# A hybrid encoder trunk on one core: gates and branch projections with tokens stationary and 512 weight columns moving

## The chip, the cores and the metric

One NeuronCore of a Trainium2 chip runs the whole kernel. The metric is the device time in microseconds (us) from the start to the end of one execution; lower is better. Engines are named as the profile does: PE is the matrix engine TensorE, with PEld its loads of stationary operands; DVE is VectorE, ACT is ScalarE, POOL is GpSimd, and SP is the engine whose queue issues most DMAs. SBUF is the on-chip working memory of 128 partitions, PSUM the small accumulation memory that PE writes.

## What is computed

Two layers act on 256 tokens of 1,024 features, all in fp32. In each layer four token mixers (three attentions and a convolution) give four branches of 256 features. What this case is about is the joining of the four:

```python
proj = jnp.einsum('bsnc,ncd->bsnd', branches, w_branch)
gates = jax.nn.sigmoid(h @ w_gate + b_gate).reshape(b, s, N_BRANCH, D_MODEL)
x = x + jnp.sum(gates * proj, axis=2) @ w_o

hf = rms_norm(x, g_ffn)
x = x + jnp.square(jax.nn.relu(hf @ w_up)) @ w_down
```

Here `h` is the RMS-normed input, `w_gate` has 1,024 x 4,096 entries, `w_branch` four times 256 x 1,024, and `w_o` 1,024 x 1,024.

## The kernel before

**Weights and matmuls.** All weights are streamed, in tiles of 128 partitions x 1,024 floats (512 KB). `weights` (L102) loads such a tile by a DMA of SP into `raw` (five buffers), lets ACT round it to `hi` (L114) and DVE subtract to `lo = raw - hi` (L115); `hi` and `lo` have four buffers each. While `share[1]` is 2, which is so during attention, every second `lo` is made by POOL. Activations are split into the same two parts. A product is three matmuls (`mm3`, L120 to L124): high by high, and the two mixed ones, in a reduced-precision type. Whichever operand is stationary has 128 columns; the other one moves.

**Gates.** `gates(g)` (L712) makes two blocks of 128 output features for all 256 tokens: the weights are stationary, the 256 tokens of `xg` move, eight blocks of the contraction and three matmuls each, 24 per weight tile (`mtile`, L341). DVE multiplies the two blocks by the tokens' norm factor (L717) into `Z`, which holds features in the partitions; `sigmoids` (L719) adds the bias as a per-partition scalar and applies the sigmoid on ACT.

**Branches.** `branch(m)` (L724) does the four projections of one block of 128 output features, 24 matmuls of 256 moving tokens. DVE multiplies them by the gates (L737), POOL adds the four in two steps (L738, L739), ACT and DVE split the sum into its two parts `y` (L740, L741), which stand ready as the stationary operand of the output projection.

**Output projection.** From L779 on, tokens are stationary and 512 columns of `w_o` move (`tokens`, L761), 12 matmuls per weight tile, accumulated in four PSUM tiles `po`; the result is added to the stream `X` (`joined`, L771), and `to_features` (L296) turns X by fp32 transposes for the MLP.

**Order.** PE's instructions run in the order in which the program names them. The other engines' and the DMA queue's orders are set at build time by a scheduler that gives each engine, in program order of priority, what its model says is ready; an engine then runs its list in that order. During attention, `tick` (L333) is called behind each weight tile and runs the next list of steps of `side`: scores, transposes and weighted values of a head, pieces of the convolution. There are 31 such lists per layer, 13 of them used up before the gates begin, so 18 gate tiles share PE with attention. Behind that, L744 to L758 put one `branch` after each `gates`.

**PSUM.** There are eight banks: four `mm` (pool `pmm`, through `new_ps`), one `sc` for scores, one `pv` for weighted values, and two `ms` for transposes and small things.

Of the kernel before, what the change touches and what calls it, by code (L numbers as in the profile page):

```python
# [17 lines left out]
F32 = mybir.dt.float32  # L18
# [6 lines left out]
P = 128  # L25
# [17 lines left out]

C_GMIX, C_GFFN, C_BGATE, C_GQ, C_GKV, C_DW, C_BDW, C_GLN, C_BLN, C_BF = 0, 8, 16, 48, 50, 51, 113, 115, 117, 119
NSMALL = 123

# [23 lines left out]
@with_exitstack  # L70
def hybrid_trunk(ctx: ExitStack, tc: tile.TileContext, xT, xtok, pos, small, gfin, abias, w_lat, w_v, w_in, w_uq, w_ukv,
                 w_gate, w_br, w_o, w_up, w_dn, out):
# [17 lines left out]
    def nm(s):  # L90
        count[0] += 1
        return f"{s}_{count[0]}"
# [33 lines left out]
    def cols(pair, i):  # L126
        return pair[0][:, i * P:(i + 1) * P], pair[1][:, i * P:(i + 1) * P]
# [197 lines left out]
    for l in range(L):  # L325
        s = sm[l]

        def col(c):
            return s[:, c:c + 1]
# [377 lines left out]


        Z = [big.tile([P, 16, T], F32, tag="big", name=nm("Z")) for _ in range(2)]
        y = [None, None]  # L710

        def gates(g):  # L712
            ps = new_ps("pgt")
            for i in range(2):
                mtile(ps[:, i * T:(i + 1) * T], w_gate[l, 2 * g + i], xg)
            i = 2 * g % 16
            nc.vector.tensor_tensor(Z[g // 8][:, i:i + 2, :], ps2(ps), bc(rb, 2), op=ALU.mult)  # L717

        def sigmoids(m):  # L719
            for i in range(4 * m, 4 * m + 4):  # L720
                zt = Z[i // 16][:, i % 16, :]
                after(nc.scalar.activation(zt, zt, AF.Sigmoid, bias=col(C_BGATE + i)), last_exp[0])

        def branch(m):  # L724
            if m == 0:
                y[:] = [act.tile([P, 8, T], F32R, tag="qk1", name=nm("yh")),
                        act.tile([P, 8, T], F32R, tag="qk2", name=nm("yl"))]
            w = weights(w_br[l, m])
            yt = tmp.tile([P, 4, T], F32, tag="y4", name=nm("yt"))
            for a in range(2):  # L730
                ps = new_ps("pbr")
                for n in range(2):
                    for k in range(2):
                        i = 2 * (2 * a + n) + k
                        mm3(ps[:, n * T:(n + 1) * T], cols(w, i), part(br, i), k == 0, k == 1)
                i = (4 * m + 2 * a) % 16
                nc.vector.tensor_tensor(yt[:, 2 * a:2 * a + 2, :], ps2(ps), Z[m // 4][:, i:i + 2, :], op=ALU.mult)  # L737
            nc.gpsimd.tensor_tensor(yt[:, 0:2, :], yt[:, 0:2, :], yt[:, 2:4, :], op=ALU.add)  # L738
            nc.gpsimd.tensor_tensor(yt[:, 0, :], yt[:, 0, :], yt[:, 1, :], op=ALU.add)  # L739
            nc.scalar.copy(y[0][:, m, :], yt[:, 0, :])  # L740
            nc.vector.tensor_tensor(y[1][:, m, :], yt[:, 0, :], y[0][:, m, :], op=ALU.subtract)  # L741

        nbr = -1
        for g in range(16):  # L744
            gates(g)
            if side:
                continue
            share[1] = 0
            if nbr < 0:
                conv_silu(last_exp[0])  # L750
            else:
                branch(nbr)
            nbr += 1
            sigmoids(nbr)
        for m in range(nbr, KT):
            branch(m)
            if m + 1 < KT:
                sigmoids(m + 1)  # L758


        def tokens(ps, st, w, j, first, last):  # L761
# [3 lines left out]
        def block(pair, k, b):  # L765
            return pair[0][:, k, b * P:(b + 1) * P], pair[1][:, k, b * P:(b + 1) * P]

        xg2 = new_xg()
        po = {(b, h): new_ps("po") for h in range(2) for b in range(NB)}

# [4 lines left out]

        def gffn(k):
            return col(C_GFFN + k)

        for kp, h in ((0, 0), (0, 1), (1, 0), (1, 1), (2, 0), (2, 1), (3, 0), (3, 1)):  # L779
            w = weights(w_o[l, kp, h])  # L780
            for b in range(NB):
                for j in range(2):
                    k = 2 * kp + j
                    tokens(po[b, h], block(y, k, b), w, j, k == 0, k == KT - 1)
                if kp == 3:
                    joined(b, h)
# [176 lines left out]
```

## Time and profile before

| | |
|---|---|
| median of three runs | 844.81 us (844.40 to 846.23) |
| the profiled execution | 843.17 us |
| its span in the trace | 841.4 us |
| mean granted clock of PE | 0.998 of full |
| PE, DVE, ACT, POOL busy | 98%, 68%, 53%, 18% of the span |
| bytes moved by DMA | 145.55 MB, 173 GB/s on average |

The span is what the trace covers; the execution's own time has 1.8 us around it. Busy shares are averages over stages with different limits, and a PE shown busy is not PE at its peak, since its matmuls are pipelined and overlap in the records. Start-to-start distances tell its pace.

### The profile page before, as it was taken

The numbers are of one execution on the slowest core, as the hardware profiler recorded it, in microseconds if no ns is written. First come the engines' busy times: TensorE is split into PE (matmuls) and PEld (weight loads), VectorE is DVE, ScalarE is ACT, GpSimd is POOL, SyncE is SP. The second block draws the span as 40 slices with busy tenths as digits, with TensorE's granted clock in tenths as the row PEclk, the third lists the DMA queues.
The fourth block names the chain that finished last, engine by engine and source line by source line (L and its number), as shares of the span: only waits on it lengthen the run. The fifth ranks groups of instructions, "written<-read, shape, count | busy, mean of one in ns | idle before, by whom it ended". The sixth has DMA issues, their size and how long they took to land.

```text
span 841.4 us, 14516 instructions
## 1 busy us (share of the span) xinstructions
PE 823.5 (98%) x5646; PEld 757.9 (90%) x5646; DVE 570.1 (68%) x948; ACT 449.5 (53%) x757; POOL 153.0 (18%) x156
## 2 busy tenths in 40 slices
PE   8999999999999999999999999999999999999996
PEld 7879999999889999999899899999998899999995
DVE  7899984787675555555578899557866655555554
ACT  6755546654464444444485664485445554545443
POOL 6534232133200000000014332312331000000000
PEclk9999999999999999999999999999999999999999
DMA  8765343455556555656554534345555555555531
GB/s 278 223 211 173 125 140 128 160 184 192 161 165 201 179 196 181 193 181 197 165 174 160 190 129 149 130 133 173 193 176 200 174 183 194 188 189 181 194 127 50
DMA packets 42549, 145.55 MB, mean 173 GB/s; under 512 B 5104, under 2 KB 7408, under 8 KB 42352
## 3 DMA queue, kind: packets, MB, share of 16 engines
q1 hardware_dynamic: 41904, 142.98, 52.7%
q10 hardware_dynamic: 576, 1.64, 0.6%
q8 instruction: 44, 0.72, 0.4%
q14 instruction: 25, 0.20, 0.1%
HBM read 143.55 MB, written 1.05 MB: 172 GB/s over the span
## 4 chain that ended last, share of the span: by engine, by line
PE 91%; DVE 5%; issue 2%; POOL 1%; DMA 1%; ACT 0%; SPq 0%; POOLq 0%; DVEq 0%; ACTq 0%
PE pgt L122 7%; PE pgt L123 7%; PE pgt L124 7%; PE pu L123 7%; PE pu L124 7%; PE pd L123 7%; PE pu L122 7%; PE pd L122 7%; PE pd L124 7%; PE S L555 2%; DVE lo L115 2%; PE pqk L122 2%; PE pPV L593 2%; PE pqk L123 2%; PE pqk L124 2%; PE po L122 2%
## 5 line engine op out<-in xcount | busy, mean ns | idle before, releaser
L115 DVE TENSOR_TENSOR lo<-raw,hi 128x1024 fp32r<-128x1024 f32 (+3 forms) x241 | 298.4, 1241 | 196.6 <-ACT hi L114 194.4
L114 ACT CAST hi<-raw 128x1024 fp32r<-128x1024 f32 (+2 forms) x273 | 278.4, 1024 | 266.9 <-issue 208.7
L122 PE MATMUL pgt<-xgh,hi 128*128 128x256 f32 x512 | 149.5, 292 | 0.0
L122 PE MATMUL pu<-xgh,hi 128*128 128x256 f32 x512 | 144.9, 283 | 0.7 <-ACT xgh L293 0.7
L123 PE MATMUL pu<-xgl,hi 128*128 128x256 f32 x512 | 145.1, 283 | 0.3
L124 PE MATMUL pu<-xgh,lo 128*128 128x256 f32 x512 | 144.9, 283 | 0.0
L123 PE MATMUL pgt<-xgl,hi 128*128 128x256 f32 x512 | 144.7, 283 | 0.0
L124 PE MATMUL pgt<-xgh,lo 128*128 128x256 f32 x512 | 144.7, 283 | 0.0
L123 PE MATMUL pd<-hi,u 128*128 128x512 f32 x256 | 100.5, 393 | 1.1 <-DVE u L804 1.1
L122 PEld LDWEIGHTS pu<-xgh,hi 128*128 128x128 f32 x512 | 98.0, 191 | 3.4 <-ACT xgh L293 1.1
L122 PE MATMUL pd<-hi,u 128*128 128x512 f32 x256 | 100.7, 393 | 0.4 <-ACT u L803 0.4
L123 PEld LDWEIGHTS pu<-xgl,hi 128*128 128x128 f32 x512 | 98.0, 191 | 3.0 <-DVE xgl L294 0.7
L124 PE MATMUL pd<-lo,u 128*128 128x512 f32 x256 | 99.6, 389 | 0.0
L122 PEld LDWEIGHTS pgt<-xgh,hi 128*128 128x128 f32 x512 | 97.9, 191 | 0.8 <-issue 0.3
L123 PEld LDWEIGHTS pgt<-xgl,hi 128*128 128x128 f32 x512 | 98.1, 192 | 0.4
L124 PEld LDWEIGHTS pu<-xgh,lo 128*128 128x128 f32 x512 | 98.0, 191 | 0.0
L124 PEld LDWEIGHTS pgt<-xgh,lo 128*128 128x128 f32 x512 | 97.9, 191 | 0.0
L115 POOL TENSOR_TENSOR lo<-raw,hi 128x1024 fp32r<-128x1024 f32 (+1 forms) x32 | 77.2, 2414 | 110.7 <-ACT hi L114 106.1
L491 DVE SCALAR_TENSOR_TENSOR cacc<-up,sm,cacc 128x256 f32<-128x256 f32 x120 | 77.4, 689 | 0.0
L124 PEld LDWEIGHTS pd<-lo,u 128*128 128x128 f32 x256 | 48.1, 188 | 10.4
L123 PEld LDWEIGHTS pd<-hi,u 128*128 128x128 f32 x256 | 48.3, 189 | 9.4 <-DVE u L804 1.7
L122 PEld LDWEIGHTS pd<-hi,u 128*128 128x128 f32 x256 | 48.3, 189 | 9.2 <-ACT u L803 0.8
(254 smaller groups left out, 1356.8 us busy)
## 6 DMA issues: line engine op xcount, KB each, us to landing
raw<-in_w_gate SPq DMA_DIRECT2D x64, 512.0 KB, 3.8
raw<-in_w_up SPq DMA_DIRECT2D x64, 512.0 KB, 4.1
raw<-in_w_dn SPq DMA_DIRECT2D x64, 512.0 KB, 3.9
raw<-in_w_in SPq DMA_DIRECT2D x23, 512.0 KB, 4.2
raw<-in_w_br SPq DMA_DIRECT2D x16, 512.0 KB, 3.6
raw<-in_w_o SPq DMA_DIRECT2D x16, 512.0 KB, 4.4
raw<-in_w_v SPq DMA_DIRECT2D x8, 512.0 KB, 4.3
raw<-in_w_lat SPq DMA_DIRECT2D x8, 210.0 KB, 4.9
```

Source lines behind the costliest of these rows:

```text
L114: cut = nc.scalar.copy(hi[:, c:c + w], raw[:, c:c + w])
L115: done = eng.tensor_tensor(lo[:, c:c + w], raw[:, c:c + w], hi[:, c:c + w], op=ALU.subtract)
L122: nc.tensor.matmul(ps, sh, mh, start=first, stop=False)
L123: nc.tensor.matmul(ps, *((sl, mh) if late_mov else (sh, ml)), start=False, stop=False)
L124: nc.tensor.matmul(ps, *((sh, ml) if late_mov else (sl, mh)), start=False, stop=last)
L491: ins = nc.vector.scalar_tensor_tensor(cacc[:, c, :], up[:, c, j:j + T], wcol, cacc[:, c, :], op0=ALU.mult, op1=ALU.add)
L555: nc.tensor.matmul(sl, q[:, b * P:(b + 1) * P], k[:, 0:n], start=True, stop=True)
L593: nc.tensor.matmul(po[o:o + 64, 0:T], v[:, 0, vo:vo + HD], pts[:, 0:T], start=True, stop=False)
```

## The change

Gates and branch projections change operands: the tokens become stationary (128 at a time, two blocks `b`) and 512 weight columns move, as the output projection does already. The weights are laid out for it on the host. `gates(c, i)` makes the gate of branch `i` for the half `c` of the output features from four weight tiles, with `tick` behind each of them; DVE scales by the per-token norm factor and adds the bias in one operation. As the bias now lies along the free axis, it comes as a tile of 128 x 512 floats (256 KB) per gate by a DMA of its own, into one buffer, and leaves the table `small`, which shrinks from 123 to 91 columns. `sigmoids(c)` runs over 1,024 elements per partition. `branch(c, i)` projects one branch onto 512 features of both token blocks, in PSUM banks of the `sc`, `pv` and `ms` pools; DVE multiplies into `Z` in place; POOL adds the branches 1 and 2 to the sum in `Z[c][:, 0]`, DVE adds branch 3. The sum has tokens in its partitions, so `turned(c)` turns it by 8 fp32 transposes per half into `y`, copied by ACT and subtracted by DVE. The last four branch tiles are interleaved with output tiles. The core of the diff (numbering of the table's columns and some of the host's layout left out):

```diff
-def hybrid_trunk(ctx: ExitStack, tc: tile.TileContext, xT, xtok, pos, small, gfin, abias, w_lat, w_v, w_in, w_uq, w_ukv,
+def hybrid_trunk(ctx: ExitStack, tc: tile.TileContext, xT, xtok, pos, small, gfin, bgate, abias, w_lat, w_v, w_in, w_uq, w_ukv,
...
@@ -705,80 +705,99 @@
         qk(4, True)
         qk(6, False)
 
-
-        Z = [big.tile([P, 16, T], F32, tag="big", name=nm("Z")) for _ in range(2)]
-        y = [None, None]
-
-        def gates(g):
-            ps = new_ps("pgt")
-            for i in range(2):
-                mtile(ps[:, i * T:(i + 1) * T], w_gate[l, 2 * g + i], xg)
-            i = 2 * g % 16
-            nc.vector.tensor_tensor(Z[g // 8][:, i:i + 2, :], ps2(ps), bc(rb, 2), op=ALU.mult)
-
-        def sigmoids(m):
-            for i in range(4 * m, 4 * m + 4):
-                zt = Z[i // 16][:, i % 16, :]
-                after(nc.scalar.activation(zt, zt, AF.Sigmoid, bias=col(C_BGATE + i)), last_exp[0])
-
-        def branch(m):
-            if m == 0:
+        def tokens(ps, st, w, j, first, last):
+
+            mm3(ps, st, (w[0][:, j * 512:(j + 1) * 512], w[1][:, j * 512:(j + 1) * 512]), first, last, late_mov=True)
+
+        def block(pair, k, b):
+            return pair[0][:, k, b * P:(b + 1) * P], pair[1][:, k, b * P:(b + 1) * P]
+
+
+        Z = [big.tile([P, 4, NB, 512], F32, tag="big", name=nm("Z")) for _ in range(2)]
+        y = []
+
+        def gates(c, i):
+            ps = [new_ps("pgt") for _ in range(NB)]
+            bg = tmp.tile([P, 512], F32, tag="bg", name=nm("bg"), bufs=1)
+            for kp in range(4):
+                w = weights(w_gate[l, c, i, kp])
+                if kp == 0:
+                    nc.sync.dma_start(bg, bgate[l, c, i])
+                for b in range(NB):
+                    for j in range(2):
+                        k = 2 * kp + j
+                        tokens(ps[b], block(xg, k, b), w, j, k == 0, k == KT - 1)
+                tick()
+            for b in range(NB):
+                nc.vector.scalar_tensor_tensor(Z[c][:, i, b, :], ps[b], rc[:, b:b + 1], bg, op0=ALU.mult, op1=ALU.add)
+
+        def sigmoids(c):
+            for i in range(4):
+                after(nc.scalar.activation(Z[c][:, i], Z[c][:, i], AF.Sigmoid), last_exp[0])
+
+        def branch(c, i):
+            pools = (((psc, "sc"), (ppv, "pv")), ((pms, "ms"), (pms, "ms")))[i % 2]
+            ps = [pool.tile([P, 512], F32, tag=tag, name=nm("pbr")) for pool, tag in pools]
+            w = weights(w_br[l, c, i])
+            for b in range(NB):
+                for j in range(2):
+                    tokens(ps[b], block(br, 2 * i + j, b), w, j, j == 0, j == 1)
+                nc.vector.tensor_tensor(Z[c][:, i, b, :], ps[b], Z[c][:, i, b, :], op=ALU.mult)
+                if i == 3:
+                    nc.vector.tensor_tensor(Z[c][:, 0, b, :], Z[c][:, 0, b, :], Z[c][:, 3, b, :], op=ALU.add)
+            if i in (1, 2):
+                nc.gpsimd.tensor_tensor(Z[c][:, 0], Z[c][:, 0], Z[c][:, i], op=ALU.add)
+
+        def turned(c):
+
+            if c == 0:
                 y[:] = [act.tile([P, 8, T], F32R, tag="qk1", name=nm("yh")),
                         act.tile([P, 8, T], F32R, tag="qk2", name=nm("yl"))]
-            w = weights(w_br[l, m])
-            yt = tmp.tile([P, 4, T], F32, tag="y4", name=nm("yt"))
-            for a in range(2):
-                ps = new_ps("pbr")
-                for n in range(2):
-                    for k in range(2):
-                        i = 2 * (2 * a + n) + k
-                        mm3(ps[:, n * T:(n + 1) * T], cols(w, i), part(br, i), k == 0, k == 1)
-                i = (4 * m + 2 * a) % 16
-                nc.vector.tensor_tensor(yt[:, 2 * a:2 * a + 2, :], ps2(ps), Z[m // 4][:, i:i + 2, :], op=ALU.mult)
-            nc.gpsimd.tensor_tensor(yt[:, 0:2, :], yt[:, 0:2, :], yt[:, 2:4, :], op=ALU.add)
-            nc.gpsimd.tensor_tensor(yt[:, 0, :], yt[:, 0, :], yt[:, 1, :], op=ALU.add)
-            nc.scalar.copy(y[0][:, m, :], yt[:, 0, :])
-            nc.vector.tensor_tensor(y[1][:, m, :], yt[:, 0, :], y[0][:, m, :], op=ALU.subtract)
-
-        nbr = -1
-        for g in range(16):
-            gates(g)
+            for pr in range(2):
+                pt = pms.tile([P, 512], F32, tag="ms", name=nm("pyt"))
+                for j in range(2):
+                    o = (2 * pr + j) * P
+                    for b in range(NB):
+                        nc.tensor.transpose(pt[:, j * T + b * P:j * T + (b + 1) * P], Z[c][:, 0, b, o:o + P], ident)
+                ks = slice(4 * c + 2 * pr, 4 * c + 2 * pr + 2)
+                nc.scalar.copy(y[0][:, ks, :], ps2(pt))
+                nc.vector.tensor_tensor(y[1][:, ks, :], ps2(pt), y[0][:, ks, :], op=ALU.subtract)
+
+        todo = [(0, i) for i in range(4)]
+        for c, i in [(c, i) for c in range(2) for i in range(4)]:
+            gates(c, i)
             if side:
                 continue
-            share[1] = 0
-            if nbr < 0:
+            if share[1]:
+                share[1] = 0
                 conv_silu(last_exp[0])
-            else:
-                branch(nbr)
-            nbr += 1
-            sigmoids(nbr)
-        for m in range(nbr, KT):
-            branch(m)
-            if m + 1 < KT:
-                sigmoids(m + 1)
-
-
-        def tokens(ps, st, w, j, first, last):
-
-            mm3(ps, st, (w[0][:, j * 512:(j + 1) * 512], w[1][:, j * 512:(j + 1) * 512]), first, last, late_mov=True)
-
-        def block(pair, k, b):
-            return pair[0][:, k, b * P:(b + 1) * P], pair[1][:, k, b * P:(b + 1) * P]
+                sigmoids(0)
+                continue
+            for _ in range(2):
+                if todo:
+                    branch(*todo.pop(0))
+                    if not todo:
+                        turned(0)
+        sigmoids(1)
+        for t in todo:
+            branch(*t)
+        if todo:
+            turned(0)
+
 
         xg2 = new_xg()
-        po = {(b, h): new_ps("po") for h in range(2) for b in range(NB)}
+        po = {}
 
         def joined(b, h):
 
             xs = X[:, b, h * 512:(h + 1) * 512]
             nc.vector.tensor_tensor(xs, po[b, h], xs, op=ALU.add)
 
-        def gffn(k):
-            return col(C_GFFN + k)
-
-        for kp, h in ((0, 0), (0, 1), (1, 0), (1, 1), (2, 0), (2, 1), (3, 0), (3, 1)):
+        def output(kp, h):
             w = weights(w_o[l, kp, h])
             for b in range(NB):
+                if kp == 0:
+                    po[b, h] = new_ps("po")
                 for j in range(2):
                     k = 2 * kp + j
                     tokens(po[b, h], block(y, k, b), w, j, k == 0, k == KT - 1)
@@ -786,6 +805,21 @@
                     joined(b, h)
                     if (h, b) == (1, 0):
                         to_features(0, xg2, gffn, pms, "ms")
+
+        def gffn(k):
+            return col(C_GFFN + k)
+
+        branch(1, 0)
+        output(0, 0)
+        branch(1, 1)
+        output(0, 1)
+        branch(1, 2)
+        branch(1, 3)
+        output(1, 0)
+        output(1, 1)
+        turned(1)
+        for kp, h in ((2, 0), (2, 1), (3, 0), (3, 1)):
+            output(kp, h)
         v2 = stream_squares()
         rsq = tmp.tile([P, NB], F32, tag="rsq", name=nm("rsq"))
         nc.vector.reciprocal(rsq, v2)
...
-    gate = A(w_gate).reshape(L, KT, P, 4, KT, P).transpose(0, 4, 3, 2, 1, 5).reshape(L, 32, P, D)
-    bgate = A(b_gate).reshape(L, 4, KT, P).transpose(0, 3, 2, 1).reshape(L, P, 32)
-    brw = A(w_branch).reshape(L, 4, 2, P, KT, P).transpose(0, 4, 3, 1, 2, 5).reshape(L, KT, P, D)
+    gate = A(w_gate).reshape(L, 4, 2, P, 4, 2, 512).transpose(0, 5, 4, 1, 3, 2, 6).reshape(L, 2, 4, 4, P, D)
+    bgate = A(b_gate).reshape(L, 4, 2, 512).transpose(0, 2, 1, 3)[:, :, :, None, :]
+    bgate = np.broadcast_to(bgate, (L, 2, 4, P, 512))
+    brw = A(w_branch).reshape(L, 4, 2, P, 2, 512).transpose(0, 4, 1, 3, 2, 5).reshape(L, 2, 4, P, D)
...
```

## Rows read from the trace of the kernel before

**Rows 1.** The page: busy time by engine; the last chain by engine.

```profile
PE 823.5 (98%) x5646; PEld 757.9 (90%) x5646; DVE 570.1 (68%) x948; ACT 449.5 (53%) x757; POOL 153.0 (18%) x156
...
PE 91%; DVE 5%; issue 2%; POOL 1%; DMA 1%; ACT 0%; SPq 0%; POOLq 0%; DVEq 0%; ACTq 0%
```

**Rows 2.** Busy time by window, no attention: length, engines, PEclk, DMA share, GB/s.

```profile
160.00:210.00 50.00, 50.00 (x419) 50.00 (x418) 37.98 (x40) 24.35 (x35) 17.60 (x12) 1.00 0.57 186
```

**Rows 3.** The timeline of PE: start us, us, engine, line, instruction, count.

```profile
57.93 0.50 PE L122 MATMUL pv<-hi,xgh 128*128 128x512 f32 x1
...
60.79 0.49 PE L582 MATMUL pT<-ident,pe 128*128 128x128 f32 x3
...
82.68 0.47 PE L122 MATMUL pgt<-xgh,hi 128*128 128x256 f32 x1
...
85.74 0.49 PE L582 MATMUL pT<-ident,pe 128*128 128x128 f32 x3
...
190.09 0.28 PE L123 MATMUL pgt<-xgl,hi 128*128 128x256 f32 x1
190.22 0.28 PE L124 MATMUL pgt<-xgh,lo 128*128 128x256 f32 x1
```

**Rows 4.** The chain, end of the output projection: start us, us, what.

```profile
234.68 0.23 PE po L122
...
237.40 0.87 PE pt L303 x8
```

**Rows 5.** PE's waits, whole span: us in total, times, longest us.

```profile
PE S L555 <- DVE qkA L636: 1.9, 1, 1.9
...
PE po L122 <- DVE yt L737: 0.6, 2, 0.3
```

**Rows 6.** The chain, start of the output projection.

```profile
214.86 2.15 POOL yt L738
...
218.64 0.69 DVE yt L737
```

**Rows 7.** The page's groups, and the view of tile pbr.

```profile
L122 PE MATMUL pgt<-xgh,hi 128*128 128x256 f32 x512 | 149.5, 292 | 0.0
...
L122 PE MATMUL pbr<-brh,hi x128: 283/283/284, 158.7 to 626.5; 128*128 128x256 f32 x128
```

**Rows 8.** Groups of DVE by shape: count, busy us, mean ns, idle before.

```profile
L737 DVE TENSOR_TENSOR yt<-pbr,Z 128x512 f32<-128x512 f32 x32 | 20.7, 683 | 0.1
...
L829 DVE SCALAR_TENSOR_TENSOR X<-pd,rsq,X 128x512 f32<-128x512 f32 x8 | 6.0, 748 | 4.6 <-PE pd L124 4.6
...
L525 DVE TENSOR_TENSOR xc<-xc,dsg 128x512 f32<-128x512 f32 x2 | 1.4, 682 | 0.0
```

**Rows 9.** Groups of POOL by shape.

```profile
L115 POOL TENSOR_TENSOR lo<-raw,hi 128x1024 fp32r<-128x1024 f32 x30 | 74.6, 2489 | 110.3 <-ACT hi L114 105.7 <-DVE qn L418 4.6
```

**Rows 10.** The timelines of DVE and of POOL, free stretch.

```profile
168.65 1.21 DVE L115 TENSOR_TENSOR lo<-raw,hi 128x1024 fp32r<-128x1024 f32 x1
...
171.38 2.14 DVE L115 TENSOR_TENSOR lo<-raw,hi 128x1024 fp32r<-128x1024 f32 x1 [0.31 <-ACT hi L114]
...
171.15 1.29 POOL L738 TENSOR_TENSOR yt<-yt 128x512 f32<-128x512 f32 x1 [5.67 <-DVE yt L737]
```

**Rows 11.** The timeline of ACT, free stretch.

```profile
158.78 1.05 ACT L114 CAST hi<-raw 128x1024 fp32r<-128x1024 f32 x1 [1.83 <-PE pgt L123]
```

**Rows 12.** Groups of ACT by shape.

```profile
L650 ACT ACTIVATE VAC<-pv,rc 128x512 f32<-128x512 f32 x4 | 2.8, 695 | 1.8 <-PE pv L124 1.8
```

**Rows 13.** The timeline of SP's queue.

```profile
44.59 5.03 SPq L110 DMA_DIRECT2D raw<-in_w_in  x3
53.16 0.33 SPq L558 DMA_DIRECT2D bt<-in_abias  x1
```

**Rows 14.** The page's DMA issues: size of one, us to landing.

```profile
raw<-in_w_gate SPq DMA_DIRECT2D x64, 512.0 KB, 3.8
```

More of the change, by code (lines that the diff above doesn't have):

```diff
@@ L42 @@
 WCOLS = 1024
-C_GMIX, C_GFFN, C_BGATE, C_GQ, C_GKV, C_DW, C_BDW, C_GLN, C_BLN, C_BF = 0, 8, 16, 48, 50, 51, 113, 115, 117, 119
-NSMALL = 123
+C_GMIX, C_GFFN, C_GQ, C_GKV, C_DW, C_BDW, C_GLN, C_BLN, C_BF = 0, 8, 16, 18, 19, 81, 83, 85, 87
+NSMALL = 91
 A0 = 4
@@ L706, in hybrid_trunk @@
         qk(6, False)
-        Z = [big.tile([P, 16, T], F32, tag="big", name=nm("Z")) for _ in range(2)]
-        y = [None, None]
-        def gates(g):
-            ps = new_ps("pgt")
-            for i in range(2):
-                mtile(ps[:, i * T:(i + 1) * T], w_gate[l, 2 * g + i], xg)
-            i = 2 * g % 16
-            nc.vector.tensor_tensor(Z[g // 8][:, i:i + 2, :], ps2(ps), bc(rb, 2), op=ALU.mult)
-        def sigmoids(m):
-            for i in range(4 * m, 4 * m + 4):
-                zt = Z[i // 16][:, i % 16, :]
-                after(nc.scalar.activation(zt, zt, AF.Sigmoid, bias=col(C_BGATE + i)), last_exp[0])
-        def branch(m):
-            if m == 0:
-                y[:] = [act.tile([P, 8, T], F32R, tag="qk1", name=nm("yh")),
-                        act.tile([P, 8, T], F32R, tag="qk2", name=nm("yl"))]
-            w = weights(w_br[l, m])
-            yt = tmp.tile([P, 4, T], F32, tag="y4", name=nm("yt"))
-            for a in range(2):
-                ps = new_ps("pbr")
-                for n in range(2):
-                    for k in range(2):
-                        i = 2 * (2 * a + n) + k
-                        mm3(ps[:, n * T:(n + 1) * T], cols(w, i), part(br, i), k == 0, k == 1)
-                i = (4 * m + 2 * a) % 16
-                nc.vector.tensor_tensor(yt[:, 2 * a:2 * a + 2, :], ps2(ps), Z[m // 4][:, i:i + 2, :], op=ALU.mult)
-            nc.gpsimd.tensor_tensor(yt[:, 0:2, :], yt[:, 0:2, :], yt[:, 2:4, :], op=ALU.add)
-            nc.gpsimd.tensor_tensor(yt[:, 0, :], yt[:, 0, :], yt[:, 1, :], op=ALU.add)
-            nc.scalar.copy(y[0][:, m, :], yt[:, 0, :])
-            nc.vector.tensor_tensor(y[1][:, m, :], yt[:, 0, :], y[0][:, m, :], op=ALU.subtract)
-        nbr = -1
-        for g in range(16):
-            gates(g)
-            if side:
-                continue
-            share[1] = 0
-            if nbr < 0:
-                conv_silu(last_exp[0])
-            else:
-                branch(nbr)
-            nbr += 1
-            sigmoids(nbr)
-        for m in range(nbr, KT):
-            branch(m)
-            if m + 1 < KT:
-                sigmoids(m + 1)
         def tokens(ps, st, w, j, first, last):
@@ new lines, in turned @@
+        def turned(c):
+            if c == 0:
+                y[:] = [act.tile([P, 8, T], F32R, tag="qk1", name=nm("yh")),
+                        act.tile([P, 8, T], F32R, tag="qk2", name=nm("yl"))]
+            for pr in range(2):
[7 more added lines that the diff above has]
+                nc.vector.tensor_tensor(y[1][:, ks, :], ps2(pt), y[0][:, ks, :], op=ALU.subtract)
@@ new lines, in hybrid_trunk @@
+        todo = [(0, i) for i in range(4)]
+        for c, i in [(c, i) for c in range(2) for i in range(4)]:
+            gates(c, i)
+            if side:
+                continue
+            if share[1]:
+                share[1] = 0
+                conv_silu(last_exp[0])
+                sigmoids(0)
+                continue
+            for _ in range(2):
[3 more added lines that the diff above has]
+                        turned(0)
@@ L943 @@
     bf = np.broadcast_to(A(b_forget)[:, None, :], (L, P, HEADS))
-    small = np.concatenate([pk(g_mix), pk(g_ffn), bgate, pk(g_q_lat), pk(g_kv_lat), dw, pk(b_dw), pk(g_conv_ln),
+    small = np.concatenate([pk(g_mix), pk(g_ffn), pk(g_q_lat), pk(g_kv_lat), dw, pk(b_dw), pk(g_conv_ln),
                             pk(b_conv_ln), bf], axis=2)
@@ L951 @@
         xT=A(x).reshape(T, KT, P).transpose(2, 1, 0), xtok=A(x).reshape(NB, P, D).transpose(1, 0, 2), pos=A(positions).reshape(NB, P).T, small=small,
-        gfin=np.broadcast_to(A(g_final)[None], (P, D)), abias=abias, w_lat=wlat, w_v=wv, w_in=win_t, w_uq=uq, w_ukv=ukv, w_gate=gate,
+        gfin=np.broadcast_to(A(g_final)[None], (P, D)), bgate=bgate, abias=abias, w_lat=wlat, w_v=wv, w_in=win_t, w_uq=uq, w_ukv=ukv, w_gate=gate,
         w_br=brw, w_o=wo, w_up=wt(w_up), w_dn=dn)
```

## The prediction

> **What bounds the kernel now.** I began with the busy shares and the shares of the chain: TensorE (PE) is busy for 98% of the span and carries 91% of the chain that ended last [rows 1]. A busy PE need not be a fast one, so I next read how far apart its instructions start. In the free stretch of gates and branches 419 matmuls of 256 columns fall into 50 us, at a granted clock of 1.00, which is the 2.4 GHz level [rows 2]: 0.119 us each. Single starts agree (190.09 and 190.22) [rows 3]; I take 0.120. The twelve matmuls of 512 columns of an output tile run from 234.68 to 237.40 [rows 4], 0.227 each. Two matmuls of 256 columns therefore cost 0.240 us where one of 512 costs 0.227: it is not that wide matmuls run faster, but that each matmul carries some 13 ns beyond its columns, and the change halves their number. Then I looked for time in which PE waits. Its whole list of waits holds nothing over 1.9 us [rows 5], and in the part that is rewritten there is one: the first output matmul waits for a chain through GpSimd, ScalarE and VectorE that ends at 219.33 [rows 6]. That is 0.3 us of standing in each layer [rows 5], or some 0.4 with PE's restart. So the engine that matters is PE, stage by stage, and everything the change adds on other engines counts only where PE has to stand.
>
> **What the change saves on PE.** Gates: 512 matmuls on each of three lines [rows 7], over two layers 1,536 of 256 columns, become 768 of 512. Branches: 128 on each line, 384 together, become 192. Per weight tile, 24 x 0.120 - 12 x 0.227 = 0.156 us. A layer has 32 gate tiles and 8 branch tiles, so 6.2 us. Next to the attention steps a few ns differ, since a plain fp32 matmul comes before and behind: 24 of 256 columns take 82.68 to 85.74, 3.06 us, and 12 of 512 columns 57.93 to 60.79, 2.86 us [rows 3], a gain of 0.20 instead. Eighteen gate tiles per layer lie there, so between nothing and 0.8 us more; I take 6.4 us per layer, bounds 6.2 to 7.0. The wait of [rows 6] should go as well, because the first output tile now stands behind a branch tile: 0.4 us per layer, bounds 0.3 to 0.5.
>
> By the Trainium skill, page "TensorE: Matmul & The Clock Gate", section "Back-to-back issue gap", an isolated matmul takes its columns over 2.4 GHz plus about 2.5 ns. By that, an estimate, the gain would be 2.5 ns for each of the 960 matmuls removed, 2.4 us in all. The starts in [rows 3, 4] are further apart than that, and the measured pace is what I use.
>
> **What it adds on PE.** Sixteen fp32 transposes per layer; eight of them take 0.87 us in the existing turn [rows 4], so 1.74 us, bounds 1.7 to 1.8.
>
> **The first turn, `turned(0)`.** It follows branch tile (0,3) directly in PE's order, and the order of PE is written out, so nothing steps in front. It needs the sum of four products. Let 0 be the moment when PE is done with (0,3). The tile before, (0,2), is done 12 x 0.227 = 2.72 us earlier. Its second product (0.683 us, as the products of L737 [rows 8]) ends near -2.0. GpSimd then adds 1,024 elements per partition: 2.49 us on average for its row of that size, and twice 1.29 us for one of half the size [rows 9, 10]; done at about +0.6. Then VectorE adds twice 512 (0.68 us each as L525, 0.6 of it net where ops follow one another) and PE is told: +2.0. That is the floor of the wait. The ceiling comes from a port that two engines don't use together: at 171.15 GpSimd adds for 1.29 us, and a `lo` that VectorE starts at 171.38 takes 2.14 instead of its usual 1.2 us, ending about 1.1 us after the add [rows 10]. Here such a `lo` is due: as soon as PE leaves a tile, ScalarE casts the next weights (the cast at 158.78, 1.05 us, had waited 1.83 us for PE [rows 11]), so the tile left at -2.72 puts a `lo` on VectorE at about -1.5, when the GpSimd add has just begun. It is held until +0.6 and done at +1.6; behind it on VectorE stand the products of (0,3) and the sums, 4 x 0.6 us: PE goes on at +4.2. Another `lo` in between would make 4.8 or more. If one product slips in front of the `lo`, 3.6. I take 3.6 us per layer, bounds 2.0 to 4.8. PE cannot make this up later, since the weights wait for PE and not PE for them.
>
> **The second turn, `turned(1)`.** Two output tiles (5.4 us) stand between branch (1,3) and it, which covers the 4.2 us above; without that cover the sum would cost what it costs at `turned(0)`. But the output tile behind it reads what it turns. The first four transposes are ready 0.6 us after the start; ScalarE copies 512 elements from PSUM (0.695 us as L650 [rows 12], a little less without a scale), VectorE subtracts 512 (0.683 as L737 [rows 8]). PE has 0.87 us of its own work and 0.227 more once the first half is there: 0.9 us of waiting at best. A weight cast of 1.05 us and a `lo` of 1.2 us become ready just ahead of the copy and of the subtraction, by the rule seen in [rows 11]; with both in front it is 2.0. I take 1.6, bounds 0.9 to 2.2.
>
> **What costs nothing, and why.** The gate epilogue becomes two operations of 0.748 us (L829's form [rows 8]) for each four weight tiles, where two multiplications of 512 stand now; a gate's PSUM is needed again only two gates later. Sigmoids: eight of 1,024 elements per layer instead of 32 of 256, off PE's path, and the last, of gate (1,3), has five tiles, 13.6 us, before its product. The bias tile adds 16 DMAs of 256 KB on SP's queue, into a single buffer: each must wait for the epilogue of the gate before. It doesn't hold up the weights queued in program order behind it, since the queue is not in program order: three weight loads of the q and k columns go out from 44.59, ahead of a bias load at 53.16 that the program names earlier and that waited for its buffer [rows 13]. A weight tile of twice the size lands in 3.8 us [rows 14], against 10.9 us of a gate. If that cover fails, see the last rival but one. Moving bias columns out of `small` shortens one small first load: nothing.
>
> **The sum.** Per layer -6.4 - 0.4 + 1.74 + 3.6 + 1.6 = +0.14 us; two layers +0.3. Against the profiled execution, 843.17 us (its span is 841.4), 843.5; the median of the runs lies 1.64 us above that execution, so 845.1 us for the median, 844.81 now. The bounds: -7.0 - 0.5 + 1.7 + 2.0 + 0.9 = -2.9 per layer (839.0), and -6.2 - 0.3 + 1.8 + 4.8 + 2.2 = +2.3 (849.4).
>
> **The rivals.**
> (1) Faster: both waits near their floors. If VectorE's order has products and sums ahead of the `lo`, `turned(0)` costs 2.2 and `turned(1)` 1.0 us; -6.4 - 0.4 + 1.74 + 2.2 + 1.0 = -1.86 per layer, so 841.1 us, down to 839.0 at the bounds. For it: VectorE is busy 38 of 50 us in the free stretch [rows 2], so there are holes. Against it: a `lo` is ready before the product by the times above.
> (2) Slower: the blocked `lo` at `turned(0)`. The place is VectorE's queue between branch (0,2) and the turn; with the `lo` ahead of both products and a second one ahead of the last sum the wait is 4.8 us or more and the second turn 2.0: +1.74 per layer, so 848.3 us. It decides from the point at which the wait there and at the second turn exceed 6.4 + 0.4 - 1.74 = 5.1 us together by 0.85 us.
> (3) The clock falls after that wait. No wait of the kernel before is longer than 1.9 us [rows 5], and the granted clock is 1.00 in the free stretch [rows 2], so no row shows what a longer one does. If one tile of 12 matmuls ran at 1.2 GHz, 12 x 0.227 = 2.7 us more per layer, 850.5 us. The Trainium skill, same page, section "What's actually happening", has TensorE fall to the lower level after idling; no run here shows it, and by that rule this rival would need a long wait first.
> (4) The bias load stands in program order on SP and holds back the weights behind it: they would start only at a gate's end, and 3.8 us landing, 1.05 cast and 1.2 `lo` against one tile of cover (2.7) leave some 4 us for each of 16 gates, 60 us more. [Rows 13] speak against it.
> (5) The change doesn't do what it says: wide matmuls with alternating stationary operands might not hold 0.227. The twelve from 57.93 to 60.79 average 0.238 [rows 3], though the switch from plain fp32 is in them. At 0.236 throughout the gain per tile falls from 0.156 to 0.05, 8.6 us less over 80 tiles: 853.7 us. The even 0.227 of the output tile [rows 4] speaks against it.
>
> **How the numbers follow.** A measurement of this kernel can tell about 0.2% (1.7 us) from no change. Forecast, within 1.7 us: 0.36. Rival 1: 0.33, all of it faster. Rival 2: 0.23; rival 3: 0.04; rival 4: 0.02; rival 5: 0.02, together 0.31 slower. The range runs from 839.5, near the floor of both waits, to 850.5, past the upper bound of the sum, to rival 3, and short of rivals 4 and 5; cases of both signs hold most of the chance, and the forecast's own range is 843.4 to 846.8.
>
> **What would show it.** Right: gate and branch matmuls 0.227 us apart, 768 and 192 of them; a wait of PE's first transpose in `turned(0)` on VectorE's Z of 2 to 5 us, and of the output tile behind `turned(1)` on ScalarE's and VectorE's y of 1 to 2 us, and no others over 1 us. Wrong: a pace away from 0.227, PE waiting for `lo` during gates, a granted clock below 1.00 after the turn, or no wait at the turns at all, which would put the time near 835 us.

## The result, and the profile after

The changed kernel takes 854.14 us, median of four runs (854.03 to 855.72); the kernel before, on the same chip, 844.61 (843.56 to 846.23). The ratio is 1.0114, 95% interval 1.0099 to 1.0129: slower by 9.5 us, above the range of the prediction. The profiled execution took 854.24 us; its span is 852.4 us against 841.4, and the mean granted clock of PE 0.987 against 0.998.

From the page of the kernel after, busy time, one group and one DMA issue:

```profile
PE 824.0 (97%) x4718; PEld 713.0 (84%) x4718; DVE 574.9 (67%) x946; ACT 438.6 (51%) x701; POOL 134.0 (16%) x134
...
L122 PE MATMUL pgt<-hi,xgh 128*128 128x512 f32 x256 | 106.3, 415 | 0.0
...
bg<-in_bgate SPq DMA_DIRECT2D x16, 256.0 KB, 3.5
```

The change did what it says: 256 gate matmuls on each line where [rows 7] had 512, and 928 fewer instructions on PE than in [rows 1]: 960 matmuls removed, 32 transposes added. PE's busy time has not fallen, for reasons that the windows and the tile below show. The gates' epilogue on VectorE never waited for `bg`. PE's longest waits after (total us, times, longest):

```profile
PE pyt L761 <- DVE Z L747: 7.0, 2, 3.5
PE S L555 <- DVE qkA L636: 2.7, 1, 2.7
PE po L123 <- DVE yl L764: 1.7, 2, 0.9
...
PE po L122 <- ACT yh L763: 1.0, 2, 0.5
...
PE pb L278 <- DVE rh L269: 0.4, 2, 0.2
```

The first line is the wait at `turned(0)`, the third and fourth that behind `turned(1)`; the wait on `yt` of [rows 5] is gone. The timeline of PE around the first turn of layer 0 (columns as in [rows 3], the idle time before an instruction and its releaser in brackets):

```profile
191.39 0.39 PE L123 MATMUL pbr<-hi,brl 128*128 128x512 f32 x1
191.62 0.39 PE L124 MATMUL pbr<-lo,brh 128*128 128x512 f32 x1
195.50 2.36 PE L761 MATMUL pyt<-ident,Z 128*128 128x128 f32 x8 [3.49 <-DVE Z L747]
197.51 0.78 PE L122 MATMUL pgt<-hi,xgh 128*128 128x512 f32 x1
198.08 0.63 PE L123 MATMUL pgt<-hi,xgl 128*128 128x512 f32 x1
198.51 0.57 PE L124 MATMUL pgt<-lo,xgh 128*128 128x512 f32 x1
198.92 0.40 PE L122 MATMUL pgt<-hi,xgh 128*128 128x512 f32 x1
```

Branch matmuls are 0.23 us apart, as forecast; then PE stands from 191.62 to 195.50, 3.88 us start to start. Behind that the first gate matmuls are 0.57, 0.43 and 0.41 apart, and full pace is back only from 198.92 on. The timelines of VectorE and of GpSimd say what it stood for:

```profile
188.61 1.41 DVE L745 TENSOR_TENSOR Z<-pbr,Z 128x512 f32<-128x512 f32 x2
190.23 3.42 DVE L115 TENSOR_TENSOR lo<-raw,hi 128x1024 fp32r<-128x1024 f32 x1 [0.21 <-ACT hi L114]
193.57 1.27 DVE L745 TENSOR_TENSOR Z<-pbr,Z 128x512 f32<-128x512 f32 x2
194.77 1.28 DVE L747 TENSOR_TENSOR Z<-Z 128x512 f32<-128x512 f32 x2
```

```profile
190.19 2.38 POOL L749 TENSOR_TENSOR Z<-Z 128x1024 f32<-128x1024 f32 x1 [11.29 <-ACT hi L114]
```

GpSimd's add begins at 190.19, the `lo` on VectorE 0.04 us later; it takes 3.42 us instead of 1.2, and behind it stand both products of (0,3) and both sums. The last sum ends at 196.05, and the second transpose starts right behind it, at 196.10. Beyond the pace of 0.227 per matmul and of 0.109 per transpose PE loses some 4.1 us. Layer 1 repeats it: 605.84 to 609.72.

The Trainium skill, page "SBUF — State Buffer", section "Who interferes with whom", says that a VectorE instruction with two SBUF inputs contends with a GpSimd instruction that reads SBUF, that the pair of ports which the two share is an exclusive lock, and that the order of issue decides who blocks. The trace agrees: 3.42 us is the 2.34 us that were left of the add, and then 1.08 us, about the length of a `lo` that nothing holds (1.22).

Where PE ran slow shows in the busy time by window (columns as in [rows 2]); first after, then the same windows before:

```profile
48.70:55.50 6.80, 6.15 (x16) 4.64 (x17) 6.76 (x20) 3.73 (x9) 0.23 (x2) 0.50 0.56 170
195.50:198.90 3.40, 3.27 (x11) 2.73 (x12) 2.76 (x4) 1.17 (x2) 0.00 (x0) 0.50 0.51 137
608.50:615.30 6.80, 5.45 (x17) 4.39 (x18) 4.29 (x6) 1.17 (x2) 0.00 (x0) 0.50 0.53 154
```

```profile
48.70:55.50 6.80, 5.56 (x28) 4.48 (x29) 6.80 (x18) 4.38 (x11) 0.56 (x1) 1.00 0.55 175
195.50:198.90 3.40, 3.40 (x31) 3.40 (x30) 3.19 (x4) 1.27 (x2) 1.58 (x2) 1.00 0.81 267
608.50:615.30 6.80, 6.80 (x59) 6.80 (x59) 5.20 (x6) 3.32 (x5) 2.20 (x2) 1.00 0.49 151
```

Apart from the last microseconds, which are slow in both kernels, three stretches after have a granted clock of 0.50, the 1.2 GHz level: one behind each first turn, and one that nothing in the diff touches, around the first scores of layer 0. PE after, then before, there:

```profile
46.30 0.39 PE L124 MATMUL pv<-lo,xgh 128*128 128x512 f32 x1
49.35 1.65 PE L555 MATMUL S<-qkA 64*128 64x128 f32 x4 [2.66 <-DVE qkA L636]
...
53.55 0.63 PE L124 MATMUL pv<-lo,xgh 128*128 128x512 f32 x1
53.98 0.63 PE L122 MATMUL pv<-hi,xgh 128*128 128x512 f32 x1
...
63.09 0.49 PE L582 MATMUL pT<-ident,pe 128*128 128x128 f32 x3
```

```profile
47.68 0.39 PE L124 MATMUL pv<-lo,xgh 128*128 128x512 f32 x1
49.94 0.92 PE L555 MATMUL S<-qkA 64*128 64x128 f32 x4 [1.87 <-DVE qkA L636]
```

After, PE came 1.4 us earlier, stood 0.8 longer for the same operand, ran matmuls 0.43 apart behind it, and left the stage at 63.09 where before left it at 60.79 [rows 3]: from 0.6 us ahead at the scores it fell 2.3 behind.

Last, a gate tile beside attention, after; [rows 3] have its counterpart at 82.68:

```profile
499.19 0.58 PE L122 MATMUL pgt<-hi,xgh 128*128 128x512 f32 x1
499.61 0.39 PE L123 MATMUL pgt<-hi,xgl 128*128 128x512 f32 x1
...
502.15 0.49 PE L582 MATMUL pT<-ident,pe 128*128 128x128 f32 x3
```

It takes 2.96 us where before took 3.06: a gain of 0.10. Behind the plain fp32 scores the first wide matmul holds the next one off for 0.42 us; the eleven others take 499.61 to 502.15, 0.231 each. The end of attention in layer 0, after and then before, gives what all 18 tiles gained: PE's lag has shrunk from 2.30 us (63.09 against 60.79) to 0.79.

```profile
153.28 0.38 PE L594 MATMUL pPV<-pts,VAC 128*64 128x128 f32 x2
```

```profile
152.49 0.38 PE L594 MATMUL pPV<-pts,VAC 128*64 128x128 f32 x2
```

### The profile page after: what moved, and what is told of

Its sections match the earlier page's. It is cut to its first block, busy times and chain, and to the rows that moved or that the text cites. A ratio compares the mean times of both kernels' runs of the same rounds, so it can differ in the third digit from the quotient of the medians.

```text
span 852.4 us, 12596 instructions
## 1 busy us (share of the span) xinstructions
PE 824.0 (97%) x4718; PEld 713.0 (84%) x4718; DVE 574.9 (67%) x946; ACT 438.6 (51%) x701; POOL 134.0 (16%) x134
## 5 line engine op out<-in xcount | busy, mean ns | idle before, releaser
L122 PE MATMUL pgt<-hi,xgh 128*128 128x512 f32 x256 | 106.3, 415 | 0.0
L115 POOL TENSOR_TENSOR lo<-raw,hi 128x1024 fp32r<-128x1024 f32 (+1 forms) x34 | 83.9, 2469 | 113.1 <-ACT hi L114 108.4
L123 PE MATMUL pgt<-hi,xgl 128*128 128x512 f32 x256 | 100.8, 394 | 0.0
L124 PE MATMUL pgt<-lo,xgh 128*128 128x512 f32 x256 | 100.7, 393 | 0.0
L491 DVE SCALAR_TENSOR_TENSOR cacc<-up,sm,cacc 128x256 f32<-128x256 f32 x120 | 73.8, 659 | 0.0
L124 PEld LDWEIGHTS pgt<-lo,xgh 128*128 128x128 f32 x256 | 48.6, 190 | 10.9
L122 PEld LDWEIGHTS pgt<-hi,xgh 128*128 128x128 f32 x256 | 48.9, 191 | 9.7 <-issue 0.3
L123 PEld LDWEIGHTS pgt<-hi,xgl 128*128 128x128 f32 x256 | 48.8, 191 | 9.4
```

The source lines that it names most:

```text
L115: done = eng.tensor_tensor(lo[:, c:c + w], raw[:, c:c + w], hi[:, c:c + w], op=ALU.subtract)
L122: nc.tensor.matmul(ps, sh, mh, start=first, stop=False)
L123: nc.tensor.matmul(ps, *((sl, mh) if late_mov else (sh, ml)), start=False, stop=False)
L124: nc.tensor.matmul(ps, *((sh, ml) if late_mov else (sl, mh)), start=False, stop=last)
L491: ins = nc.vector.scalar_tensor_tensor(cacc[:, c, :], up[:, c, j:j + T], wcol, cacc[:, c, :], op0=ALU.mult, op1=ALU.add)
```

## The experiments

"Idle matmuls" below are plain fp32 products of a constant, which nothing reads. Each is two passes of 0.112 us.

**Where the turn stands.** `turned(0)` moved behind the last gate:

```diff
                     branch(*todo.pop(0))
-                    if not todo:
-                        turned(0)
         sigmoids(1)
         for t in todo:
             branch(*t)
-        if todo:
-            turned(0)
+        turned(0)
```

> The first turn moves behind gate (1,3) in TensorE's order; nothing else changes. Theory (the wait at that turn, 4.2 us per layer, stands in the open and the slow clock follows from it): the wait goes, and so does the stretch at half clock behind it (about 1.2 us in layer 0, 2.7 in layer 1), together 12.3 us: 841.8 us. Rival (VectorE and GpSimd are behind at that point, so the wait only moves to the next branch or to the second turn): 1 to 4 us at most, 850 or more.

Measured: 840.76 us (838.65 to 843.72), ratio to before 0.9955 (0.9940 to 0.9970); run again beside a later experiment 841.65, 0.9960 (0.9945 to 0.9974). The wait is gone from the list, and the clock where it stood is 1.00:

```profile
185.00:205.00 20.00, 20.00 (x94) 16.62 (x94) 18.05 (x20) 10.31 (x11) 2.40 (x1) 1.00 0.63 202
```

That is 13.4 us below the changed kernel, and what the theory said. The profiled spans differ by 12.7 us (852.4 and 839.7): the two waits account for 8.3 of it and half clock behind them for 3.8 (the table further down); the stage of the first scores, with a slow stretch of 3.41 us instead of 6.83, is left at 62.41 instead of 63.09 and gives 0.7.

**Is the clock a cost of its own?** Idle matmuls fill the wait, so that PE does not stand: 36, then 18.

```diff
+            if c == 0:
+                idle = new_ps("idle")
+                for _ in range(36):
+                    nc.tensor.matmul(idle[:, 0:P], o256, o256, start=True, stop=True)
             for pr in range(2):
```

> 36 idle matmuls of 128 fp32 columns on constants run on TensorE just ahead of the first turn; their result is not read. Theory (the clock falls because TensorE stands still in the wait): the wait keeps its length, the granted clock stays 1.00 there, the transposes run 0.109 us apart instead of 0.213 and the gate matmuls 0.227 instead of 0.427: 3.5 us less, 850.6 us. Rival (the clock falls because fp32 transposes are too little work, or for a reason outside): no gain, 854.

Measured: 858.33 us, ratio 1.0164 (1.0144 to 1.0183). At two passes each the 36 take 8.20 us, about twice the wait. The timeline of PE:

```profile
191.74 0.40 PE L124 MATMUL pbr<-lo,brh 128*128 128x512 f32 x1
191.97 8.20 PE L759 MATMUL idle<-o 128*128 128x128 f32 x72
200.01 1.04 PE L765 MATMUL pyt<-ident,Z 128*128 128x128 f32 x8
...
201.11 0.40 PE L123 MATMUL pgt<-hi,xgl 128*128 128x512 f32 x1
```

From the last branch matmul to the first transpose it is 8.27 us instead of 3.88, 8.8 us more over two layers; the time rose by 4.2. So 4.6 us came back: about 1.0 is the second half of the sum, done by then (0.5 per layer), the rest the clock. From the first transpose to the second gate matmul it is 1.10 us here and 2.58 in layer 0 after, 0.5 of it the second half of the sum. The eight transposes take 1.04 us here, at full pace: it is not they that lower the clock.

> 18 idle matmuls instead of 36 ahead of the first turn: each fp32 matmul turned out to be two passes, 8.05 us in all, 3.9 us more than the wait. 18 take 4.0 us, as long as the wait. Theory (clock): the granted clock stays 1.00 at the turn and 3.5 us of the changed kernel's time go: 850.6. Rival: 854.

With 18, about as long as the wait itself: 848.29 us (847.14 to 849.65), ratio 1.0047 (1.0031 to 1.0062). Doing work that nobody needs made the kernel 5.9 us faster. That is more than the 3.5 expected, and the rest need not be the turn's: in this profile the clock was 1.00 in the scores' stretch as well.

```profile
40.00:60.00 20.00, 17.97 (x100) 14.63 (x100) 18.55 (x40) 10.81 (x22) 8.12 (x5) 1.00 0.71 224
185.00:205.00 20.00, 20.00 (x111) 17.20 (x110) 14.49 (x16) 6.97 (x9) 2.38 (x1) 1.00 0.52 159
```

**What makes the wait.** All sums on VectorE, so that GpSimd holds no `lo`:

```diff
-                nc.gpsimd.tensor_tensor(Z[c][:, 0], Z[c][:, 0], Z[c][:, i], op=ALU.add)
+                nc.vector.tensor_tensor(Z[c][:, 0], Z[c][:, 0], Z[c][:, i], op=ALU.add)
```

> The two sums that GpSimd makes per half go to VectorE (1,024 elements, about 1.2 us each). Theory (GpSimd's add holds the lo of VectorE for 2.2 us, and the products stand behind it): the wait at the first turn falls from 4.2 to about 2.9 us although VectorE gets more work, and no lo there is longer than 1.3 us: 2 to 5 us less with the shorter slow stretch, 849 to 852. Rival (the length of VectorE's own list sets the wait): the wait stays or grows, 854 to 857.

Measured: 853.49 us (851.49 to 855.44), ratio 1.0107 (1.0082 to 1.0132): nothing gained that can be told from the spread. PE's wait is in two parts now, as long in sum:

```profile
PE pyt L761 <- DVE Z L747: 7.3, 4, 2.0
```

VectorE has the adds in its own list, and two `lo` of 1.22 us still stand among products and sums. From the last branch matmul to the second transpose it is 4.38 us in layer 0 (190.87 to 195.25) where the changed kernel has 4.48 (191.62 to 196.10): what the held `lo` no longer costs, the longer list does. So the next run leaves the sums on GpSimd and takes only the `lo` from in front of them:

```diff
+                if (c, i) == (1, 3) and kp >= 2:
+                    after(w[2], summed[0])
```

(`w[2]` is the instruction that makes `lo`, `summed[0]` the last sum of branch (0,3).)

> After with the two roundings (lo) of the last gate tile of the group behind the last sum of branch(0,3) on VectorE, so that no rounding that GpSimd holds stands ahead of the products. If the held rounding is worth 2.2 us of the wait at turned(0) (3.42 instead of 1.23), the wait falls from 4.2 to about 2.0 us per layer and the slow-clock stretch behind it shortens or goes: 846.5 to 850. If the length of VectorE's list alone sets the wait, as the run with all sums on VectorE suggests, it stays above 3.5 us and the time at 852 or above.

Measured: 849.44 us (848.53 to 850.30), ratio 1.0046 (1.0028 to 1.0065), before on that chip 845.98. VectorE's timeline:

```profile
191.77 0.69 DVE L750 TENSOR_TENSOR Z<-Z 128x512 f32<-128x512 f32 x1 [1.22 <-POOL Z L752]
192.38 0.68 DVE L748 TENSOR_TENSOR Z<-pbr,Z 128x512 f32<-128x512 f32 x1
193.09 0.69 DVE L750 TENSOR_TENSOR Z<-Z 128x512 f32<-128x512 f32 x1
```

```profile
PE pyt L764 <- DVE Z L750: 4.7, 4, 1.3
```

From the last branch matmul to the second transpose it is now 3.05 us (190.79 to 193.84) instead of 4.48. So the held `lo` is a real part of the wait, but worth 1.4 us per layer, not 2.2: now VectorE waits for GpSimd's sum, and a product and two sums still follow it. The stretch at half clock behind the turn did not go, but is shorter in layer 1 (3.41 us instead of 6.83).

**The scores of layer 0.** 24, then 12 idle matmuls in front of them:

```diff
             mixer, h, q, k, _, _ = operands(i)
+            if l == 0 and i == 0:
+                idle = new_ps("idle")
+                for _ in range(24):
+                    nc.tensor.matmul(idle[:, 0:P], o256, o256, start=True, stop=True)
```

> 24 idle matmuls of 128 fp32 columns run on TensorE just ahead of the first scores of layer 0, where TensorE waits 2.8 us for VectorE's qkA and the clock then falls; their result is not read. Theory (this stretch at half clock, 48.7 to 55.5, costs 2.9 us and comes from the wait, which is longer than the kernel before has there): wait unchanged, clock 1.00, 2.9 us less, 851.2 us. Rival (the loss there is in VectorE's order, not in the clock): no gain, 854.

Measured: 855.47 us, ratio 1.0129 (1.0111 to 1.0148). The scores start 2.86 us later than after, at 52.21, and the stage ends at the same 63.09: the slow stretch had cost 2.9, as much as the filler put the scores off. Behind the turns half clock lasted longer than after in layer 0 (195.02 to 201.85) and shorter in layer 1 (3.41 us instead of 6.83).

> After with 12 idle plain-fp32 matmuls (24 passes of 0.112 us, 2.7 us, about the wait itself) put before the scores of layer 0. If the 2.9 us of that stretch come from the clock that falls after TensorE stands for 2.7 us, the granted clock stays 1.00 there, the matmuls start no later than in after, and the time falls by about 2.9 us, to 851.2. If the stretch costs time for another reason (the late qkA alone), it stays at 854.

Measured: 854.43 us (851.52 to 856.75), ratio 1.0108 (1.0075 to 1.0142), before on that chip 845.98. The profiled execution, with the clock at 1.00 here, is the 851.52; of the three others one, 852.94, is below the changed kernel, and 855.91 and 856.75 are above it. Not settled, so the same was put into the kernel with the later turn, where no other slow stretch can take its place, with 14 of them:

> After with turned(0) moved behind gates(1,3), as in the first experiment, and with 14 idle plain-fp32 matmuls (28 passes, about 3.1 us, as long as the wait) before the scores of layer 0; no other slow stretch is left that could take the place of this one. If the stretch at half clock behind that wait (3.41 us long in the first experiment's profile) costs time, 1.5 to 3 us go: 837.8 to 839.3. If the late operand alone sets the end of that stage, it stays at 840.8, as the same kernel without them, run beside it.

> The kernel of the first experiment once more, as the measure of the run beside it: 840.8, ratio 0.9955.

Measured: 841.04 us (840.13 to 844.17), ratio 0.9959 (0.9946 to 0.9973), against 841.65 and 0.9960 (0.9945 to 0.9974) without. The expectation of 1.5 to 3 us fell. PE with the idle matmuls, then without:

```profile
47.80 3.29 PE L554 MATMUL idle<-o 128*128 128x128 f32 x28
51.02 0.92 PE L559 MATMUL S<-qkA 64*128 64x128 f32 x4
```

```profile
50.04 0.94 PE L555 MATMUL S<-qkA 64*128 64x128 f32 x4 [3.12 <-DVE qkA L636]
...
51.83 0.63 PE L123 MATMUL pv<-hi,xgl 128*128 128x512 f32 x1
52.26 0.63 PE L124 MATMUL pv<-lo,xgh 128*128 128x512 f32 x1
```

From the first scores to the last `pv` matmul it is 10.64 us with them, 12.20 without: at full clock the stage is 1.6 us shorter. But here PE's last matmul ahead of it came 1.0 us later (47.56 against 46.54), and the idle matmuls, a fixed 3.2 us, put the scores off by as much. In all twelve executions with them the mean granted clock was 0.996 or 0.997, in the eight without it was 0.992 to 0.998: the filler steadies the clock, but no time is gained by it that can be told from the spread. How often PE comes late is not shown, since each version has one trace; so it is a guess that a filler pays only where PE's arrival is steady.

**A version without the waits.** First, with the first turn moved as above, output tile (1,1) goes behind the second turn and covers the copies of what it turns; then the convolution's pieces also start two steps later (`CONV_FROM` 4 to 6), which frees VectorE before the first scores; the last also alone on the kernel before.

```diff
         branch(1, 0)
-        output(0, 0)
         branch(1, 1)
-        output(0, 1)
+        output(0, 0)
         branch(1, 2)
         branch(1, 3)
+        output(0, 1)
         output(1, 0)
-        output(1, 1)
         turned(1)
+        output(1, 1)
```

> The first turn behind gate (1,3) as before, and the last four branch tiles in pairs, so that output tile (1,1) stands between the second turn's transposes and the first tile that reads them. Theory (the wait of 1.87 us per layer behind the second turn is ScalarE's and VectorE's time for the halves, behind a cast and a lo): the 2.72 us of the output tile cover it, 3.7 us less than with the first turn moved alone: 837.0 us. Rival (the sum itself is not ready that early, since VectorE has two branch pairs in a row): a wait of the transposes on Z comes in its place, 839 to 841.

Measured: 837.59 us (834.73 to 837.82), ratio 0.9909 (0.9888 to 0.9929): 3.2 us below the first experiment, and no wait at either turn.

> As e5, and the convolution's operations on VectorE begin two ticks later (tick 6 instead of 4). Theory (the wait ahead of the first scores of layer 0 is VectorE's: a convolution operation held by GpSimd's lo stands ahead of qkA): that wait falls from 2 to 3 us to under 1, the clock there stays 1.00, 3 to 6 us less than e5: 831 to 834. Rival (the lo of VectorE and the latents keep qkA late anyway): within 1.5 us of e5.

Measured: 834.25 us (834.00 to 834.44), ratio 0.9880 (0.9865 to 0.9894). The wait of the scores is 1.4 us and the clock 1.00 all the way:

```profile
10.00:820.00 810.00, 803.99 (x4670) 698.96 (x4671) 562.29 (x920) 428.59 (x682) 125.73 (x91) 1.00 0.59 181
```

> The kernel before with the convolution two ticks later. Theory: its wait of 1.9 us ahead of the first scores goes, no clock loss was there: 1 to 2 us less, 843. If it gains as much as e6 against e5, the slow stretch there is not part of the difference between the two kernels.

Measured: 842.41 us (841.35 to 845.13), ratio 0.9974 (0.9962 to 0.9987). The step gains 2.1 us here (844.49 before on that chip) and 3.3 in the changed kernel, whose four runs without it spread from 834.73 to 837.82; whether part of the scores' stretch belongs to the change is not settled by it. With that step on both sides, the wide projections, with both turns covered, are worth 842.41 - 834.25 = 8.2 us.

## Why the prediction was wrong

It forecast +0.3 us for two layers against the profiled execution before; the spans of the two profiled executions differ by 11.0 us. Term by term, both layers, in us:

| term | forecast | shown | from |
|---|---|---|---|
| 44 gate and branch tiles away from attention | -6.9 | -6.9 | 0.227 apart throughout |
| 36 gate tiles beside attention | -5.9 | -3.0 | lag from the first scores' end to the last weighted values: 2.30 to 0.79, in layer 1 5.98 to 4.45 |
| wait on `yt` | -0.8 | -0.9 | gone |
| 32 transposes, at full clock | +3.5 | +3.5 | 0.109 apart |
| wait at `turned(0)` | +7.2 | +8.3 | 4.1 each |
| wait behind `turned(1)` | +3.2 | +3.7 | 1.9 each |
| half clock behind `turned(0)` | 0 | +3.8 | 1.4 and 2.4 |
| scores stage of layer 0 | 0 | +2.3 | left at 63.09, not 60.79 |
| sum | +0.3 | +10.8 | |

**Right:** the pace of 0.227, the number of instructions, the bias load at no cost, both waits with their chains. At `turned(0)` the working in the text with the `lo` held in front of both products, 4.2 us, was what happened; the forecast stepped back from it to 3.6 on the chance of a better order. Behind `turned(1)` the cast (230.88) and the `lo` (231.96) did come in front, as its upper case has it.

**The step that failed first** is the one that rival (3) names: the sum put nothing for the clock behind `turned(0)`, and half clock there cost 3.8 us. The rival's price of 2.7 us per layer was somewhat high, with 1.4 and 2.4 shown, and its chance of 0.04 far too low. The text excused it because "no row shows what a longer" wait does; but it forecast 3.6 us itself, twice the longest wait in [rows 5], so the unknown belonged into the sum or into the upper bound. The Trainium skill, page "TensorE: Matmul & The Clock Gate", section "What's actually happening", has TensorE at the lower level after idling; every run here in which PE stood at the first turn agrees, with 0.50 granted behind it, and those in which it did not stand there have 1.00.

**The second** is the term for the tiles beside attention. "A gain of 0.20" was taken from a `pv` tile, whose fp32 neighbours are others: from the first of the four scores ahead of it to its first matmul it is 0.85 us (57.08 to 57.93), ahead of a gate tile 0.57, before and after (82.11 to 82.68, 498.62 to 499.19), so 0.28 of its switch from fp32 stood outside the 2.86. Between gate tiles the switch costs the same, some 0.19 over the pace (0.42 to the next start wide, 0.31 narrow), but the wide ones behind it stand 0.231 apart, not 0.227. So 0.10 to 0.11 per tile, and a new wait on `rh`, 0.2 us in the list, by which the lag grows by 0.46 in each layer (in layer 0 from 148.72 against 148.28 to 149.90 against 149.00). The bounds, 6.2 to 7.0, allowed for no loss beside attention, though no row showed a wide gate tile there. The versions without waits at the turns agree roughly with these terms: -6.9 - 3.0 - 0.9 + 3.5 = -7.3 us, against the 8.2 measured between the last two runs above.

**The third** was not in the text at all: a stage that the diff does not touch. PE reached the scores earlier and stood longer for the same operand. The orders of VectorE, GpSimd and ScalarE up to there are the same in both kernels; what differs is which of two `lo` began first, VectorE's or GpSimd's. After, then before:

```profile
37.91 5.75 POOL L115 TENSOR_TENSOR lo<-raw,hi 128x1024 fp32r<-128x1024 f32 x2
38.27 3.12 DVE L115 TENSOR_TENSOR lo<-raw,hi 128x1024 fp32r<-128x1024 f32 x1
```

```profile
38.69 1.22 DVE L115 TENSOR_TENSOR lo<-raw,hi 128x1024 fp32r<-128x1024 f32 x1
38.89 5.67 POOL L115 TENSOR_TENSOR lo<-raw,hi 128x1024 fp32r<-128x1024 f32 x2
```

Two of GpSimd's stand in one line. After, VectorE's took 3.12 us behind GpSimd's first; before it took 1.22, and the convolution's next step 4.50. The traces of all fourteen versions fall into these two ways: in four VectorE's `lo` is not behind and takes 1.22 us, in ten GpSimd's begins first, by as little as 0.04 us, and VectorE's takes 2.3 to 3.4. Two versions with the change (the `lo` behind the sums, and the 14 idle matmuls) went the way of before, so the diff does not fix it; both kernels without the change went that way too, so that the change shifts the odds is not excluded. The idle matmuls show that half clock costs this stage 1.6 to 2.9 us when it happens; whether it does varies by execution, as the next section shows, so the table's 2.3 us is true of two executions and not of the medians. The 1.64 us that the forecast added for the typical execution already holds most of it: medians differ by 9.5, profiled spans by 11.0.

Rival (1) fell with the waits near their upper ends; rivals (4) and (5) fell on `bg` (3.5 us to landing, no wait) and on the pace; rival (2) was half right, with waits of 6.0 us together, over its limit of 5.1 by 0.9 as it asked, and in each layer 1.9 us of clock and 1.5 of attention on top.

## What to carry to other kernels

On an engine that is busy for 98%, price a new wait twice: once for the time that it stands, once for the matmuls behind it at half clock, which here was half as much again. Before a dependent turn is put into an in-order stream, look for independent tiles to put between producer and turn: one gate of four tiles here took 13 us off. And ask of a profiled execution how it stands to the others of its kernel before a small term is read off it.

## What the hardware showed

The length of a wait alone did not tell whether the clock falls. A wait of 1.87 us for the scores before was followed by 1.00; a wait of 1.88 us at the same place, in the run with the `lo` behind the sums, by a stretch at half clock from 50.60 to 54.02; one of 2.0, in the run with 18 idle matmuls at the turn, by 1.00 again. The six longer ones that no idle matmuls filled, 2.6 to 3.4 us in as many traces, were all followed by a stretch at half clock. What decides in the shorter ones stays open.

The kernel before has such stretches too, though its profiled execution shows none between start and end. Its mean granted clock was noted for each of 54 executions beside the experiments: in the 10 with 0.997 or more the median time is 842.85 us, in the 19 with 0.996 it is 844.71, in the 7 with 0.992 it is 846.39. The profiled one, at 0.998 and 843.17 us, was among the first. Where the others lose it was not seen, for want of a trace. The wait before the scores is the longest of the kernel, and the version in which it is 1.4 us and no turn is waited for spread over 0.44 us in its four runs, the changed kernel's over 1.7. But the kernel before with the convolution later, whose wait there is 1.1 us, still spread from 841.35 to 845.13 in ten runs at mean clocks of 0.994 to 0.998, and its slowest run is the profiled one, at 0.998: the clock is not all that varies.
